# All products of one superchunk before the other, in the first tile of an MLP's up projection

## The chip, the core and the metric

The kernel runs on one core of a Trainium2 chip. The metric is the device time of one execution in microseconds. The engines are TensorE (PE, matrix products), VectorE (DVE), ScalarE (ACT), GpSimd (POOL) and SyncE (SP, which here only issues transfers). Each works through a queue of instructions in a fixed order and waits at semaphores.

## The reference

One layer of a decoder with two mixers, then an MLP, on 1024 prompt tokens and 64 decode tokens (1088 together). Cut to what matters here:

```
h = x + concat([o_r, o_s], axis=-1) @ w_out
hf = rms_norm(h, norm_ffn_gain)
h = h + jnp.square(jax.nn.relu(hf @ w_up)) @ w_down
```

The width is 1024, that of the MLP 4096. All inputs and outputs are float32.

## The kernel before

The tokens are cut into two superchunks of 544 (s = 0 and 1), each with two halves of Q = 272. After the mixers comes the output projection with the residual, superchunk 0 and then 1; `residual` puts h aside, multiplies it by the gain (tile f) and sums its squares (acc). The factor 1/rms is not multiplied into the operand. It is applied behind the up projection: `act` computes max(x, 0) times rsf, and its square on ACT.

The MLP's products follow the scheme with seven products for a 2x2 block product. `up(fp)` computes 256 columns of w_up, fp from 0 to 15 (a tile of up). Its left factors are sums and differences of the four quadrants of the weights: product 1 takes the first quadrant, 2 the second, 4 the fourth, and 5, 6, 7, 3 take combinations (wu0_s5, wu0_s6, ...), which POOL forms in `left`. `wsplit` then splits each into a high part, cast on ACT, and a low part, subtracted on DVE (wu0_w6 is the factor of product 6 of tile 0). The order of the products is `PROD = (1, 2, 6, 5, 7, 4, 3)`. The right operands (op_0h, op_0l for superchunk 0, op_1h, op_1l for 1) are made by `operands` from f and stay for all sixteen tiles.

One product for one superchunk is four times `mm3`, the three matmuls hi x hi, lo x hi, hi x lo: 12 matmuls of 272 columns. Each superchunk has three accumulators in PSUM, psx, psy and psz. Products 1, 6, 7 and 4 add up one after another in psx, 2 stands in psy, 5 and 3 in psz. After 1, 6 and 7 ACT copies the running sum out (tiles m1, m6, m7, shown as m); DVE adds psy or psz to these copies and calls act.

The loads of the weights' halves (wu_r) are issued by ACT's queue, into three buffers; the split factors have four buffers of each of two kinds (wa, wb). The first two factors of tile 0 are made ahead, with the last residuals.

The 1/rms of superchunk s is made in two steps. `norm(s)` sums acc over the partitions with 24 small matmuls (psr), scales on DVE (into rst for s = 0, nsinks for s = 1) and takes the power -1/2 on POOL. `norm_spread(s)` spreads the result over the partitions with six matmuls against the identity (psn), which ACT copies to rsf. For superchunk 0 both lie between residuals of superchunk 1; for superchunk 1 both lie in the first tile of up.

The order of each engine's queue is not simply that of the code: a planner with its own estimate of times sets it, under the dependencies of the code. It runs when the kernel is built.

Of the kernel before, what the change touches and what calls it, by code (L numbers as in the profile page):

```python
# [11 lines left out]
F32 = mybir.dt.float32  # L12
F32R = mybir.dt.float32r
AF = mybir.ActivationFunctionType
ALU = mybir.AluOpType
# [5 lines left out]
P = 128  # L21
# [3 lines left out]
Q = 272  # L25
# [11 lines left out]
def hymba_layer(ctx: ExitStack, tc: tile.TileContext, a: dict, o: dict):  # L37
    nc = tc.nc
# [68 lines left out]
    ident = cload("ident")  # L107
# [21 lines left out]
    u_d = [scratch.tile([P, 2, 2, 7, Q], F32, name=f"u_d{g}") for g in range(8)]  # L129
# [47 lines left out]
    def mm3(ps, lh, ll, rh, rl, first, last, more=False):  # L177
        nc.tensor.matmul(ps, lh, rh, start=first, stop=False, skip_group_check=more)  # L178
        nc.tensor.matmul(ps, ll, rh, start=False, stop=False, skip_group_check=more)  # L179
        nc.tensor.matmul(ps, lh, rl, start=False, stop=last, skip_group_check=more)  # L180
# [120 lines left out]
    for c, (c0, cw) in enumerate(CH):  # L301
        acc = rsb[:, c0 : c0 + cw]
# [4 lines left out]
    w = wload(a["w_in"][2], 8, "wkv", "v")  # L307
# [462 lines left out]
        return raw  # L770


    mix, acc, fs = {}, {}, {}

    def mix_load(s, pl):
        for x, d_ in zip("hl", (ms_hi_d, ms_lo_d)):
# [15 lines left out]
    def out_half(s, half, ps, h, w, first, last):  # L792
        for k in range(4):
            lh, ll = (w[:, i, k * 128 : k * 128 + 128] for i in range(2))
            mh, ml = (mix[s, half + x][:, k, h, :] for x in "hl")
            mm3(ps, lh, ll, mh, ml, first and k == 0, last and k == 3)

    def residual(s, m, pss):
        y = om.tile([P, 2, Q], F32, tag="y", name=f"y{s}_{m}", bufs=2)
# [53 lines left out]
    def norm(s):  # L853

        ps = psM.tile([P, 512], F32, tag="b", name=f"psr{s}")
        for h in range(2):
            for i, r in enumerate((0, 128, 144)):
                col_sums(ps[:, 3 * h + i : 3 * h + i + 1], acc[s][:, h, r : r + 128], ones[:, 0:1])
        rf = (rst, nsinks)[s][:, 0:6]
        nc.vector.tensor_scalar(rf, ps[:, :6], 1.0 / 1024.0, EPS, ALU.mult, ALU.add)  # L860
        rsqrt_inplace(rf, 6)

    def norm_spread(s):
        rf = (rst, nsinks)[s][:, 0:6]
        for h in range(2):
            pb = psM.tile([P, 512], F32, tag="b", name=f"psn{s}{h}")
            for i, (c0, n) in enumerate(((0, 128), (128, 128), (256, 16))):
                nc.tensor.matmul(
                    pb[:, c0 : c0 + n], rf[:, 3 * h + i : 3 * h + i + 1].broadcast_to([P, 128]), ident[:, 128 - n :],
                    start=True, stop=True,  # L870
                )
            nc.scalar.copy(rsf[:, s, h, :], pb[:, :Q])  # L872


# [12 lines left out]
    held = {}  # L887
# [104 lines left out]
    for ms in ((0, 1), (2, 3), (4, 5), (6, 7)):  # L992
        if ms[0] > 3:
            out_parts(1, ms, "a", late, pss)
        out_parts(1, ms, "r", late, pss)
        if ms == (6, 7):
            gen0 = left(PROD, a["w_up"][0], "wu0", nc.vector, tags=("wa", "wa", "wb", "wb"))
            ready = [next(gen0), next(gen0)]
        for m in ms:
            residual(1, m, [pss[m, h] for h in range(2)])  # L1000
            if rest:
                operands(0, rest.pop(0))
            operands(1, m)
        if ms == (2, 3):
            norm(0)
        if ms == (4, 5):
            norm_spread(0)
    ox.close()


# [4 lines left out]
    def up(fp):  # L1015
        gen = chain(ready, gen0) if fp == 0 else left(
            PROD, a["w_up"][fp], f"wu{fp}", nc.vector, tags=("wa", "wa", "wb", "wb"))
        x, y, z = ([bank(f"ps{n}{s}") for s in range(2)] for n in "xyz")
        home = {1: (x, True), 2: (y, True), 6: (x, False), 5: (z, True), 7: (x, False), 4: (x, False), 3: (z, False)}
        ra, rb = ([um.tile([P, n, Q], F32, tag=f"r{n}{s}", name=f"r{n}t{fp}_{s}") for s in range(2)] for n in (3, 4))  # L1020
        held, wait = {}, []

        def tq(n, s):
            return um.tile([P, Q], F32, tag="tq", name=f"{n}{fp}_{s}", bufs=9)

        def add(n, s, bank_):
            t_ = held[n, s]
            nc.vector.tensor_tensor(t_, t_, bank_, ALU.add)
            return t_

        def act(t_, src, s, h, dst):

            nc.vector.scalar_tensor_tensor(t_, src, 0.0, rsf[:, s, h, :], ALU.max, ALU.mult)  # L1033
            nc.scalar.activation(dst, t_, AF.Square)

        for i in PROD:
            w = next(gen)
            for s in range(2):
                bk, first = home[i][0][s], home[i][1]
                for k in range(4):  # L1040
                    lh, ll = (w[:, j, k * 128 : k * 128 + 128] for j in range(2))
                    rh, rl = (ops[RIGHT[i]][s][j][:, k, :] for j in range(2))
                    mm3(bk, lh, ll, rh, rl, first and k == 0, k == 3, not first)
                if i in (1, 6, 7):
                    t_ = held[i, s] = tq(f"m{i}", s)
                    nc.scalar.copy(t_, bk)
                if i == 2:
                    t_ = add(1, s, bk)
                    wait.append((t_, t_, s, 0, ra[s][:, B11, :]))
                    if fp or s == 0:  # L1050
                        act(*wait.pop())
                    else:
                        norm(1)
                if i == 6 and s == 1 and wait:
                    norm_spread(1)
                if i == 7:
                    if wait:
                        act(*wait.pop())
                    t_ = add(7, s, z[s])
                    act(t_, t_, s, 1, ra[s][:, B22, :])  # L1060
                if i == 4:
                    act(tq("v", s), bk, s, 0, ra[s][:, B21, :])
                    nc.sync.dma_start(u_d[fp // 2][:, fp % 2, s, :3, :], ra[s])
                if fp == 15 and s == 1 and i == 2:
                    first_down(1, ("1h", "1l", "2h", "2l"))
                if fp == 15 and s == 1 and i == 5:
                    first_down(6, ("6h", "6l", "5h", "5l"))
                if i == 3:
                    t_ = add(6, s, bk)
                    r12 = um.tile([P, Q], F32, tag="r12", name=f"r12{fp}_{s}", bufs=2)  # L1070
                    act(t_, t_, s, 1, r12)
                    b11, b21, b22 = (ra[s][:, i_, :] for i_ in (B11, B21, B22))
                    t1, t2, t3, t4 = (rb[s][:, i_, :] for i_ in range(4))
                    sub = lambda o_, p_, q_: nc.gpsimd.tensor_tensor(o_, p_, q_, ALU.subtract)  # L1074
                    sub(t1, r12, b11)
                    sub(t2, b22, t1)
                    sub(t4, b21, t2)
                    sub(t3, b22, r12)
                    nc.sync.dma_start(u_d[fp // 2][:, fp % 2, s, 3:, :], rb[s])

    begun, raws1 = {}, []

# [198 lines left out]
```

## Time and profile before

| | |
|---|---|
| median of 3 runs | 1247.72 us (1240.08 to 1247.75) |
| profiled execution | 1244.97 us, span 1243.2 us |
| PE busy | 1199.7 us, 97% of the span |
| DVE, POOL, ACT busy | 69%, 45%, 41% |
| granted clock of PE, mean | 0.982 |

The profiled execution is one of its own beside the three runs. Its span counts from the first to the last instruction. A row of an engine's timeline may stand for several instructions (x3), with the time from the first start to the last end. The first tile of up begins at 530.32 us.

### The profile page before, as it was taken

To read this page: it belongs to the slowest core of one execution; us is meant where nothing else is said; L and a number is where in the kernel's file an instruction comes from. 1 tells how busy PE (TensorE), PEld (TensorE's weight loads), DVE (VectorE), ACT (ScalarE), POOL (GpSimd) and SP (SyncE) were. 2 spreads that over 40 slices of the span, in tenths; PEclk is the share of its full clock that TensorE was granted. 3 is DMA by queue.
4 is the path that set the end of the run, shared out by engine and by line. 5 is a ranking of instruction groups with operands and counts; after the bars stand their busy time and mean duration, and the time that the engine had idled before them with its cause. 6 is when DMAs were issued, how large, how long until landed. Compare 5 with 4: busy or idle time off the path is not lost.

```text
span 1243.2 us, 23934 instructions
## 1 busy us (share of the span) xinstructions
PE 1199.7 (97%) x9621; PEld 1153.0 (93%) x9621; DVE 851.7 (69%) x1508; ACT 507.9 (41%) x1035; POOL 553.5 (45%) x463
## 2 busy tenths in 40 slices
PE   7999999999998999969999999999889999999998
PEld 6999888888888999869999999999889999999998
DVE  8856667643136888778666676766378778897776
ACT  6343434573124425444444444444363424233331
POOL 8425333332225646467666666666472231253000
PEclk9999999999899999979999999999989999999999
DMA  6211235232415753523434343445664445553215
GB/s 235 70 59 65 82 104 159 91 100 75 120 52 181 220 162 114 166 79 141 152 129 150 135 149 135 142 151 176 202 227 144 159 144 175 197 176 125 73 55 180
DMA packets 102277, 169.46 MB, mean 136 GB/s; under 512 B 11999, under 2 KB 68255, under 8 KB 101911
## 3 DMA queue, kind: packets, MB, share of 16 engines
q1 hardware_dynamic: 89335, 124.35, 30.0%
q10 hardware_dynamic: 10272, 34.67, 8.8%
q0 software_dynamic: 2560, 8.91, 2.3%
q8 instruction: 75, 1.23, 0.4%
q14 instruction: 35, 0.29, 0.1%
HBM read 114.30 MB, written 53.61 MB: 135 GB/s over the span
## 4 chain that ended last, share of the span: by engine, by line
PE 56%; DVE 6%; DMA 2%; issue 2%; POOL 1%; ACT 1%; ACTq 0%; DVEq 0%; POOLq 0%
PE psd L179 8%; PE psd L178 8%; PE psd L180 8%; PE psx L178 5%; PE psx L179 5%; PE psx L180 5%; PE psz L178 2%; PE psz L180 2%; PE psz L179 2%; PE pso L178 1%; PE pso L180 1%; PE pso L179 1%; DVE op_0l L755 1%; PE psy L178 1%; PE psy L180 1%
## 5 line engine op out<-in xcount | busy, mean ns | idle before, releaser
L178 PE MATMUL psd<-uh,wd_w 128*128 128x272 f32 x896 | 258.7, 290 | 8.0 <-ACT wd_w L754 4.5
L179 PE MATMUL psd<-uh,wd_w 128*128 128x272 f32 x896 | 260.1, 291 | 0.2 <-DVE wd_w L755 0.2
L180 PE MATMUL psd<-ul,wd_w 128*128 128x272 f32 x896 | 258.6, 289 | 0.0
L178 PEld LDWEIGHTS psd<-uh,wd_w 128*128 128x128 f32 x896 | 169.9, 190 | 9.0 <-ACT wd_w L754 4.7
L179 PEld LDWEIGHTS psd<-uh,wd_w 128*128 128x128 f32 x896 | 169.7, 189 | 0.5 <-DVE wd_w L755 0.5
L180 PEld LDWEIGHTS psd<-ul,wd_w 128*128 128x128 f32 x896 | 169.6, 189 | 0.0
L1151 DVE TENSOR_TENSOR a<-a,psd 128x272 f32<-128x272 f32 x248 | 101.5, 430 | 43.0 <-PE psd L180 42.9
L755 DVE TENSOR_TENSOR wu_w<-wu_s,wu_w 128x512 fp32r<-128x512 f32 x64 | 64.3, 1009 | 53.8 <-ACT wu_w L754 53.2
L755 DVE TENSOR_TENSOR ul<-ur,uh 128x1088 fp32r<-128x1088 f32 x56 | 82.2, 1493 | 11.3 <-ACT uh L754 11.3
L754 ACT CAST wd_w<-wd_s 128x512 fp32r<-128x512 f32 x64 | 37.4, 618 | 119.1 <-PE psd L180 104.5
L178 PE MATMUL psx<-op_0h,wu_w 128*128 128x272 f32 x256 | 75.2, 294 | 7.1 <-ACT wu_w L754 5.2
L180 PE MATMUL psx<-op_0l,wu_w 128*128 128x272 f32 x256 | 74.9, 293 | 0.0
L178 PE MATMUL psx<-op_1h,wu_w 128*128 128x272 f32 x256 | 74.8, 292 | 0.0
L179 PE MATMUL psx<-op_0h,wu_w 128*128 128x272 f32 x256 | 74.7, 292 | 0.0
L180 PE MATMUL psx<-op_1l,wu_w 128*128 128x272 f32 x256 | 74.5, 291 | 0.0
L179 PE MATMUL psx<-op_1h,wu_w 128*128 128x272 f32 x256 | 74.2, 290 | 0.0
L366 POOL TENSOR_TENSOR sp<-sp,ssp 128x1024 f32<-128x1024 f32 (+1 forms) x16 | 28.6, 1787 | 100.4 <-DVE ssp L365 95.7
L1033 DVE SCALAR_TENSOR_TENSOR m<-m,rsf 128x272 f32<-128x272 f32 x96 | 69.3, 722 | 3.2 <-ACT rsf L872 0.6
L754 ACT CAST uh<-ur 128x1088 fp32r<-128x1088 f32 x56 | 59.5, 1099 | 17.8 <-PE psd L179 9.1
L1074 POOL TENSOR_TENSOR r4t<-r3t,r4t 128x272 f32<-128x272 f32 x64 | 64.6, 1019 | 1.2
L755 DVE TENSOR_TENSOR wd_w<-wd_s,wd_w 128x512 fp32r<-128x512 f32 x64 | 52.4, 832 | 16.8 <-ACT wd_w L754 16.8
L178 PE MATMUL psf<-hnh,wqk_hi 128*128 128x384 f32 (+1 forms) x192 | 63.3, 330 | 0.0
(328 smaller groups left out, 3809.2 us busy)
## 6 DMA issues: line engine op xcount, KB each, us to landing
ur<-u_d SPq DMA_DIRECT2D x54, 544.0 KB, 5.0
u_d<-r4t SPq DMA_DIRECT2D x32, 544.0 KB, 4.5
wu_r<-in_w_up ACTq DMA_DIRECT2D x32, 512.0 KB, 4.2
wd_r<-in_w_down ACTq DMA_DIRECT2D x30, 512.0 KB, 5.3
u_d<-r3t SPq DMA_DIRECT2D x32, 408.0 KB, 2.9
y<-in_xY POOLq DMA_DIRECT2D x16, 272.0 KB, 3.1
y_d<-y POOLq DMA_DIRECT2D x16, 272.0 KB, 3.5
yt<-y_d SPq DMA_DIRECT2D x16, 272.0 KB, 3.8
```

The costliest lines, as they stand in the source:

```text
L178: nc.tensor.matmul(ps, lh, rh, start=first, stop=False, skip_group_check=more)
L179: nc.tensor.matmul(ps, ll, rh, start=False, stop=False, skip_group_check=more)
L180: nc.tensor.matmul(ps, lh, rl, start=False, stop=last, skip_group_check=more)
L366: nc.gpsimd.tensor_tensor(s, s, ss.unsqueeze(2).broadcast_to([P, 4, n]), ALU.mult)
L754: nc.scalar.copy(hi, src)
L755: lo_eng.tensor_tensor(lo, src, hi.bitcast(F32), ALU.subtract)
L1033: nc.vector.scalar_tensor_tensor(t_, src, 0.0, rsf[:, s, h, :], ALU.max, ALU.mult)
L1074: sub = lambda o_, p_, q_: nc.gpsimd.tensor_tensor(o_, p_, q_, ALU.subtract)
L1151: nc.vector.tensor_tensor(to, to, ps, ALU.add)
```

## The change

In the first tile (fp = 0) the loop runs over all seven products for superchunk 0 and then over all seven for superchunk 1; the other fifteen tiles keep the order of product by product, both superchunks each. `norm(1)` is called behind product 5 of superchunk 0, and `norm_spread(1)` behind product 4, with its matmuls ordered behind the last matmul of that product. `mm3` returns its last matmul for that. The holding back of superchunk 1's first act (the list `wait`) goes, since its rsf is there before. For norm_spread(0) the tie to the last matmul of the output projection's part ahead of it is new as well; it moves no instruction.

```diff
-    def norm_spread(s):
+    def norm_spread(s, ins):
...
-                nc.tensor.matmul(
+                with tc.issue_after(ins.ins):
+                    nc.tensor.matmul(
...
-        for i in PROD:
-            w = next(gen)
-            for s in range(2):
...
-                if i == 2:
-                    t_ = add(1, s, bk)
-                    wait.append((t_, t_, s, 0, ra[s][:, B11, :]))
-                    if fp or s == 0:
-                        act(*wait.pop())
-                    else:
-                        norm(1)
-                if i == 6 and s == 1 and wait:
-                    norm_spread(1)
-                if i == 7:
-                    if wait:
-                        act(*wait.pop())
...
+        order = [(i, s) for s in range(2) for i in PROD] if fp == 0 else [(i, s) for i in PROD for s in range(2)]
...
+        for i, s in order:
+            if i not in ws:
+                ws[i] = next(gen)
+            w = ws[i]
...
+                ins = mm3(bk, lh, ll, rh, rl, first and k == 0, k == 3, not first)
...
+            if i == 2:
+                t_ = add(1, s, bk)
+                act(t_, t_, s, 0, ra[s][:, B11, :])
+            if fp == 0 and s == 0 and i == 5:
+                norm(1)
+            if fp == 0 and s == 0 and i == 4:
+                norm_spread(1, ins)
```

What the planner makes of it is seen in the queues. On PE the first tile begins with products 1 and 2 of superchunk 0; then come the first matmuls of products 6 and 5, fourteen of the 24 sums, the rest of 6 and 5, the other ten sums, products 7, 4 and 3, the spreading, and superchunk 1 with 1, 2, 5, 6, two blocks of tile 1's product 1, then 7, two blocks of tile 1's product 2, then 4 and 3. From tile 2's second product on, all queues hold the same rows as before.

ACT, from the first copy out of psx in tile 0, before (the number behind a name is the buffer's; m10_0 is the copy after product 1 for superchunk 0, wu1_w1 the factor of product 1 of tile 1):

```order
L1046 COPY m10_0_6086<-psx0_6064 128x272
L1046 COPY m10_1_6100<-psx1_6065 128x272
L1034 ACTIVATE r3t0_0_6070<-m10_0_6086 128x272
L754 CAST wu0_w6_6161<-wu0_s6_6159 128x512
L754 CAST wu0_w5_6202<-wu0_s5_6157 128x512
L754 CAST wu0_w7_6231<-wu0_s7_6229 128x512
L754 CAST wu0_w4_6270<-wu0_r2_6002 128x512
L754 CAST wu1_w1_6366<-wu1_r1_6362 128x512
L754 CAST wu1_w2_6397<-wu1_r1_6362 128x512
L769 DMA wu1_r2_6364<-in_w_up 128x1024
L754 CAST wu0_w3_6307<-wu0_s3_6305 128x512
L769 DMA wu2_r1_6623<-in_w_up 128x1024
```

and ACT from the same copy now:

```order
L1050 COPY m10_0_6086<-psx0_6064 128x272
L1037 ACTIVATE r3t0_0_6070<-m10_0_6086 128x272
L754 CAST wu0_w6_6107<-wu0_s6_6105 128x512
L754 CAST wu0_w5_6124<-wu0_s5_6103 128x512
L754 CAST wu0_w7_6168<-wu0_s7_6166 128x512
L754 CAST wu0_w4_6188<-wu0_r2_6002 128x512
L754 CAST wu0_w3_6219<-wu0_s3_6217 128x512
L769 DMA wu1_r2_6364<-in_w_up 128x1024
L769 DMA wu2_r1_6623<-in_w_up 128x1024
L1050 COPY m60_0_6122<-psx0_6064 128x272
L754 CAST wu1_w6_6434<-wu1_s6_6432 128x512
L1050 COPY m70_0_6183<-psx0_6064 128x272
```

The square of superchunk 0 (the ACTIVATE) stands ahead of the casts in both; the casts of tile 1's first two factors have moved back, the load of its second half has moved up by one cast, and the cast of wu1_w6 now stands ahead of the copy m70_0.

POOL, from its last operation on the right operands (f1), before:

```order
L849 TENSOR_TENSOR f1_7_6038<-f1_7_6038,f1_3_5662 128x272
L971 TENSOR_TENSOR wu0_s5_6157<-wu0_r2_6002 128x512
L971 TENSOR_TENSOR wu0_s6_6159<-wu0_s5_6157,wu0_r1_6000 128x512
L971 TENSOR_TENSOR wu0_s7_6229<-wu0_r1_6000,wu0_r2_6002 128x512
L132 TENSOR_TENSOR nsinks_113<-nsinks_113,mhalf_111 128x6
L971 TENSOR_TENSOR wu0_s3_6305<-wu0_r1_6000,wu0_s6_6159 128x512
L971 TENSOR_TENSOR wu1_s5_6430<-wu1_r2_6364 128x512
```

and POOL from the same operation now:

```order
L849 TENSOR_TENSOR f1_7_6038<-f1_7_6038,f1_3_5662 128x272
L972 TENSOR_TENSOR wu0_s5_6103<-wu0_r2_6002 128x512
L972 TENSOR_TENSOR wu0_s6_6105<-wu0_s5_6103,wu0_r1_6000 128x512
L972 TENSOR_TENSOR wu0_s7_6166<-wu0_r1_6000,wu0_r2_6002 128x512
L972 TENSOR_TENSOR wu0_s3_6217<-wu0_r1_6000,wu0_s6_6105 128x512
L972 TENSOR_TENSOR wu1_s5_6430<-wu1_r2_6364 128x512
L972 TENSOR_TENSOR wu1_s6_6432<-wu1_s5_6430,wu1_r1_6362 128x512
L972 TENSOR_TENSOR wu1_s7_6492<-wu1_r1_6362,wu1_r2_6364 128x512
L972 TENSOR_TENSOR wu1_s3_6566<-wu1_r1_6362,wu1_s6_6432 128x512
L132 TENSOR_TENSOR nsinks_113<-nsinks_113,mhalf_111 128x6
```

The power of the second norm (nsinks) has moved behind the last combination of tile 0 and all four of tile 1.

## Rows read from the trace of the kernel before

**Rows 1.** Waits of PE, 500 to 566 us: who for whom, us in total, times, longest.

```profile
PE psx L178 <- ACT wu_w L754: 5.2, 1, 5.2
PE psy L180 <- DVE op_1l L755: 3.3, 2, 1.7
...
PE psy L178 <- ACT op_1h L754: 1.7, 1, 1.7
```

**Rows 2.** PE's timeline, first tile of up: start, us, instruction, count, idle before and releaser.

```profile
530.32 0.28 PE L178 MATMUL psx<-op_0h,wu_w 128*128 128x272 f32 x1
...
531.83 0.29 PE L178 MATMUL psx<-op_1h,wu_w 128*128 128x272 f32 x1
...
542.77 0.82 PE L158 MATMUL psr<-ones,acc 128*32 128x1 f32 x48
548.75 0.59 PE L178 MATMUL psx<-op_0h,wu_w 128*128 128x272 f32 x1 [5.16 <-ACT wu_w L754]
...
551.90 0.42 PE L180 MATMUL psx<-op_0l,wu_w 128*128 128x272 f32 x1
552.13 0.33 PE L179 MATMUL psx<-op_1h,wu_w 128*128 128x272 f32 x1
...
553.55 1.41 PE L868 MATMUL psn<-c_ident,nsinks 128*128 128x128 f32 x12
554.81 0.37 PE L178 MATMUL psz<-op_0h,wu_w 128*128 128x272 f32 x1
```

**Rows 3.** ACT's timeline there (ACTq: its DMA issues).

```profile
547.76 0.43 ACT L1034 ACTIVATE r3t<-m 128x272 f32<-128x272 f32 x1 [3.58 <-DVE m L1033]
548.09 1.64 ACT L754 CAST wu_w<-wu_s 128x512 fp32r<-128x512 f32 x3
549.64 1.66 ACT L754 CAST wu_w<-wu_r 128x512 fp32r<-128x512 f32 x3
552.34 0.33 ACTq L769 DMA_DIRECT2D wu_r<-in_w_up  x1
...
558.32 1.14 ACT L754 CAST wu_w<-wu_s 128x512 fp32r<-128x512 f32 x2 [2.60 <-POOL wu_s L971]
559.63 0.39 ACT L1046 COPY m<-psx 128x272 f32<-128x272 f32 x1 [0.17 <-PE psx L180]
```

**Rows 4.** DVE's timeline there.

```profile
540.85 5.46 DVE L755 TENSOR_TENSOR op_1l<-f,op_1h 128x272 fp32r<-128x272 f32 x6
546.22 0.77 DVE L1028 TENSOR_TENSOR m<-m,psy 128x272 f32<-128x272 f32 x2
...
548.73 2.98 DVE L755 TENSOR_TENSOR wu_w<-wu_s,wu_w 128x512 fp32r<-128x512 f32 x3 [0.93 <-ACT wu_w L754]
```

**Rows 5.** POOL's timeline there.

```profile
543.12 1.46 POOL L971 TENSOR_TENSOR wu_s<-wu_r 128x512 f32<-128x512 f32 x1
...
547.88 1.35 POOL L132 TENSOR_TENSOR nsinks<-nsinks,mhalf 128x6 f32<-128x6 f32 x1 [0.45 <-DVE nsinks L860]
...
555.63 1.29 POOL L971 TENSOR_TENSOR wu_s<-wu_r 128x512 f32<-128x512 f32 x1 [5.08 <-DMA wu_r<-in_w_up]
...
559.50 1.74 POOL L971 TENSOR_TENSOR wu_s<-wu_r,wu_s 128x512 f32<-128x512 f32 x1
```

**Rows 6.** Tile wu_r, 500 to 640 us: time of its loads from issue to landing.

```profile
DMA to landing us min/median/max: 3.2/4.1/5.7
```

**Rows 7.** PE's timeline at two other waits.

```profile
509.31 0.39 PE L178 MATMUL pso<-mixah,woa 128*128 128x272 f32 x1 [2.98 <-DVE y L802]
...
910.63 0.59 PE L178 MATMUL psd<-uh,wd_w 128*128 128x272 f32 x1 [2.15 <-ACT a L1149]
```

**Rows 8.** Windows behind these two: us, busy us (count) by engine, granted clock, DMA.

```profile
509.30:511.00 1.70, 1.69 (x13) 1.69 (x14) 1.70 (x5) 0.11 (x1) 1.10 (x2) 1.00 0.03 10
...
910.60:912.00 1.40, 1.37 (x6) 1.37 (x7) 1.40 (x2) 0.26 (x1) 1.32 (x2) 0.50 0.58 129
```

**Rows 9.** Waits of PE, 566 to 1243 us.

```profile
PE psd L178 <- ACT wd_w L754: 4.5, 1, 4.5
```

More of the change, by code (lines that the diff above doesn't have):

```diff
@@ L770, in rawload @@
         return raw
[L773 removed]
+    mix, acc, fs, last_out = {}, {}, {}, [None]
     def mix_load(s, pl):
@@ L795, in out_half @@
             mh, ml = (mix[s, half + x][:, k, h, :] for x in "hl")
-            mm3(ps, lh, ll, mh, ml, first and k == 0, last and k == 3)
+            last_out[0] = mm3(ps, lh, ll, mh, ml, first and k == 0, last and k == 3)
     def residual(s, m, pss):
@@ L1006, in hymba_layer @@
         if ms == (4, 5):
-            norm_spread(0)
+            norm_spread(0, last_out[0])
     ox.close()
@@ new lines, in up @@
+        for i, s in order:
+            if i not in ws:
+                ws[i] = next(gen)
+            w = ws[i]
+            bk, first = home[i][0][s], home[i][1]
+            for k in range(4):
+                lh, ll = (w[:, j, k * 128 : k * 128 + 128] for j in range(2))
+                rh, rl = (ops[RIGHT[i]][s][j][:, k, :] for j in range(2))
+                ins = mm3(bk, lh, ll, rh, rl, first and k == 0, k == 3, not first)
+            if i in (1, 6, 7):
+                t_ = held[i, s] = tq(f"m{i}", s)
+                nc.scalar.copy(t_, bk)
+            if i == 2:
[5 more added lines that the diff above has]
+                norm_spread(1, ins)
+            if i == 7:
+                t_ = add(7, s, z[s])
+                act(t_, t_, s, 1, ra[s][:, B22, :])
+            if i == 4:
+                act(tq("v", s), bk, s, 0, ra[s][:, B21, :])
+                nc.sync.dma_start(u_d[fp // 2][:, fp % 2, s, :3, :], ra[s])
+            if fp == 15 and s == 1 and i == 2:
+                first_down(1, ("1h", "1l", "2h", "2l"))
+            if fp == 15 and s == 1 and i == 5:
+                first_down(6, ("6h", "6l", "5h", "5l"))
+            if i == 3:
+                t_ = add(6, s, bk)
+                r12 = um.tile([P, Q], F32, tag="r12", name=f"r12{fp}_{s}", bufs=2)
+                act(t_, t_, s, 1, r12)
+                b11, b21, b22 = (ra[s][:, i_, :] for i_ in (B11, B21, B22))
+                t1, t2, t3, t4 = (rb[s][:, i_, :] for i_ in range(4))
+                sub = lambda o_, p_, q_: nc.gpsimd.tensor_tensor(o_, p_, q_, ALU.subtract)
+                sub(t1, r12, b11)
+                sub(t2, b22, t1)
+                sub(t4, b21, t2)
+                sub(t3, b22, r12)
+                nc.sync.dma_start(u_d[fp // 2][:, fp % 2, s, 3:, :], rb[s])
```

39 lines of the change are left out of this document (5 added, 34 removed).

## The prediction

> **What bounds the kernel now.** I read first who waits for whom on TensorE (PE), before and after 566 us, then the timelines of the four engines around the first tile of up. Up to there and behind it PE runs almost without a break; at this one place it has four waits, 5.2 us for a weight factor and 3.3 and 1.7 us for the right operands of superchunk 1 [rows 1], together 10.2 us. So what the change is worth must be read here.
>
> I call a block one product for one superchunk: 12 matmuls, 1.51 us at the full clock (530.32 to 531.83) [rows 2], 0.126 us a matmul. Tile 0 has 14 blocks. Before, the first four (products 1 and 2, both superchunks) and the norm's sums are done at 543.6; then PE idles until 548.75, because the third factor, w6, is not there [rows 2]. What holds w6 back is worth following. POOL begins the combinations of tile 0 at 543.12 [rows 5]. DVE splits the last right operands until 546.3, then does two additions of product 2 [rows 4]. ACT has the square of superchunk 0 ahead of the cast of w6 in its queue; this waits 3.58 us for DVE and runs at 547.76, the cast begins at 548.09, PE starts 0.66 us later [rows 3]. So ACT works strictly in its order, and w6 comes late through what stands ahead of it, not through PE. From 548.75 PE runs with matmuls 0.23 us apart until 552.13 (the lower clock), then at full rate; the spreading takes 553.55 to 554.81 [rows 2], and the eight remaining blocks of tile 0 follow without a wait: 554.81 + 8 x 1.51 = 566.9 is where tile 0's work ends (one block of tile 1 that stands between is not counted on either side).
>
> **The change part by part.**
>
> *The waits for superchunk 1's operands go.* The blocks of products 1 and 2 for superchunk 1 move behind the spreading, long after their operands. That takes away 3.3 + 1.7 us of waiting. But PE now has only two blocks before w6, not four, so it comes to w6 some 9 us earlier (533 to 534 rather than 543.6), and w6 doesn't come earlier with it. What would be late next is exactly the wait of 5.16 us, grown to some 14.
>
> *When w6 comes.* Nothing ahead of it depends on the moved blocks: POOL's, ACT's and DVE's rows up to the last right operand are the same in both orders. Only the second addition is gone from ahead of the square, half of 0.77 us [rows 4]. So the cast of w6 starts at 547.7 and PE at 548.4. The two blocks taken out of the shadow of this wait, and the sums, now have to be run after it: this is the loss.
>
> *The rest of the first pass.* From 548.4 PE does w6 and w5 with 24 sums among them. The low factor of w6 is there at about 549.4 (a subtraction takes 2.98 / 3 = 0.99 us) [rows 4]. I take the low clock (1.2 GHz) to end as much earlier as PE starts, at 551.8: ten matmuls 0.23 us apart, then twelve at 0.126, the sums 0.8: about 553.6. Product 7: 555.1. At 0.99 us each the other low factors are there at 550.4, 551.4, 552.4 and 553.4, ahead of their blocks. In ACT's queue the issue of tile 2's first load waits for the subtraction of w4 (552.4), and the copy after product 6 for this issue: 552.8, in time for product 7.
>
> *A new wait, at product 4.* Products 7 and 4 write the same bank, and with one superchunk alone they stand next to each other: product 4 can't start until ACT has copied the sum with product 7 out. Before, superchunk 1's block of 1.51 us covers that copy of 0.39 us [rows 3]. Now that copy stands in ACT's queue behind the cast of wu1_w6, tile 1's factor, which waits for POOL's second combination of tile 1, which waits for the load of tile 1's second half. Its issue: five casts of 0.55 us (1.64 / 3, 1.66 / 3) from 547.7, so 550.45, 1.9 us before the 552.34 of now. From issue to the first combination 3.29 us (552.34 to 555.63) [rows 3, 5]: 553.75. To the cast 2.69 us (558.32 - 555.63): 556.45. Cast 0.57 (half of 1.14) and copy 0.39: 557.4. So product 4 waits from 555.1 to 557.4, 2.3 us, and products 4 and 3 end at 557.4 + 3.0 = 560.4. The first 2.3 us of any error ahead of it are hidden by this wait.
>
> *The spreading.* The power of the norm on POOL now stands behind all four combinations of tile 1, not between the third and fourth of tile 0. These take 555.63 to 559.50 + 1.74 = 5.61 us, the power 1.35 [rows 5]: 553.75 + 5.61 + 1.35 = 560.7. PE waits 0.3 us for it, then spreads for 1.26: 562.0. Behind PE's waiting spread all of superchunk 1 is queued, although its matmuls don't need it.
>
> *The second pass.* Seven blocks at 1.51 = 10.6: 572.5. I add no wait: all seven factors are there; between its products 6, 7 and 4 the order puts two blocks of tile 1 each, so the copies are covered again. The first of these needs tile 1's w1 at 562.0 + 4 x 1.51 = 568.0; its buffer is free after superchunk 1's product 1 at 563.5, and copy, cast and subtraction (0.39 + 0.55 + 0.99) give 565.4, so 2.6 us to spare. Reordered stores of the result and the move of tile 2's loads cost nothing, since the blocks of tile 1 (14 x 1.51 = 21 us) cover them.
>
> **Sum.** 572.5 - 566.9 = +5.6 us; the profiled execution's 1244.97 becomes 1250.6. It lies 2.75 below the median of the three runs (1247.72), which run from 1240.08 to 1247.75; on the median the forecast is 1253.3.
>
> **Bounds.** The load is the term with the widest price: 3.2 to 5.7 us, median 4.1 [rows 6]. I take 3.29 because it is the same load at the same place, with the same second load behind it. Product 4 and the power both move with it one for one, so the sum is +5.5 to +8.0. The clock after the new 2.3 us wait is open from both sides. After a wait of 2.98 us at 509.31 it stayed at 1.00 (2.4 GHz); after one of 2.15 at 910.63 it was 0.50 [rows 7, 8]. At 0.50, twelve matmuls 0.10 us longer give +1.2; product 3 then ends behind the power, so 0.3 of it is hidden. A gain here has no row. [...]
>
> **The rivals.**
>
> *The clock falls at product 4's wait.* For it: the row at 910.63, a wait of nearly the same length. Against: the row at 509.31, a longer wait without that cost [rows 7, 8]. +5.6 + 0.9 = +6.5, or 1254.2. [...]
>
> *Faster: the waits go and none grows.* If w6 were cast by 533.3, PE would run tile 0 through: 14 x 1.51 + 0.8 + 1.26 = 23.2 us from 530.32 rather than 36.6, so 13.4 us less, 1234.3. It decides at w6: its combination would have to end 10 us before the first combination of now begins (543.12) [rows 5], and in the new order the same operations on the operands stand ahead of it on POOL. Nearly excluded. Even at half of the gap the case ends within 1%.
>
> *Absorbed.* A later wait of PE that hangs on a transfer and not on PE gives the delay back. The longest is 4.5 us, for a factor of down [rows 9]. If it is paced by something earlier than PE, +5.6 - 4.5 = +1.1, 1248.8. Against it: those factors' buffers are given free by PE's own matmuls.
>
> *Slower by 1%: tile 1's factors late.* All seven factors of tile 0 are now held until the second pass. If w1's subtraction ends after 568.0 (2.6 us later than worked out, as with a slow DVE queue behind the cast of w6), PE meets another empty place of the size of the one of now: 5.16 us and 15 matmuls 0.10 us longer, 6.7 in all. +12.3, with the clock above +13.2: 1260 to 1261.
>
> **How the numbers follow.** The sum as it stands 0.45, with the fallen clock 0.25; absorbed 0.13; tile 1's factors late 0.12; faster 0.05. Predicted 1253.3. The first two with the load's bounds reach from 1253 to 1257. The range reaches to 1246 (absorbed, and runs that lie as far below their median as the profiled execution does) and to 1260. A measurement of this kernel tells about 1% from no change, since its own three runs lie 0.6% apart. By that bound the first three cases count as the same (0.83); faster 0.05; slower 0.12.
>
> **What would show it.** In the new profile: PE idle for about 14 us from 534, ended by ACT's cast of w6 at about 548.4; no wait for op_1; a wait of some 2 us at the block of psx with w4, ended by ACT's copy or cast, with ACT itself waiting for POOL, and POOL for a load; the spreading ended by POOL's power at about 560.7; then no wait until tile 2. It is wrong if w6's cast comes much earlier than 548, if product 4 starts right after product 7, or if the waits behind 600 us differ from those of now.

## The result

| | before | changed |
|---|---|---|
| median of 20 runs each | 1245.61 us (1240.08 to 1249.08) | 1248.39 us (1245.99 to 1251.9) |
| span of the profiled execution | 1243.2 us | 1245.3 us |
| granted clock of PE, mean | 0.982 | 0.986 |

The changed kernel takes 1.0029 of the time before, 95% interval [1.0019, 1.0039]: 1245.61 x 0.0029 = 3.6 us more, 2.4 to 4.9. The forecast was 1253.3, from +5.6 us on a median of three runs (1247.72) that turned out 2.1 us above that of twenty. So the direction and the place were right and the size was too large: of the 4.9 us between 1253.3 and 1248.39, 2.1 lie in that base and 2.8 in the change itself.

The waits of PE from 500 to 566 us, now:

```profile
PE psx L178 <- ACT wu_w L754: 14.0, 1, 14.0
...
PE psx L178 <- ACT m L1050: 0.5, 1, 0.5
```

The three waits for superchunk 1's operands [rows 1] are gone, the one for w6 has grown from 5.2 to 14.0 us, and a new one stands at product 4. PE's timeline of the first tile:

```profile
546.09 0.59 PE L178 MATMUL psx<-op_0h,wu_w 128*128 128x272 f32 x1 [14.00 <-ACT wu_w L754]
546.61 0.59 PE L178 MATMUL psz<-op_0h,wu_w 128*128 128x272 f32 x1
547.13 0.59 PE L158 MATMUL psr<-ones,acc 128*32 128x1 f32 x28
...
551.00 0.43 PE L179 MATMUL psz<-op_0h,wu_w 128*128 128x272 f32 x1
551.22 0.39 PE L180 MATMUL psz<-op_0l,wu_w 128*128 128x272 f32 x1
...
552.30 0.36 PE L158 MATMUL psr<-ones,acc 128*32 128x1 f32 x20
552.59 0.39 PE L178 MATMUL psx<-op_0h,wu_w 128*128 128x272 f32 x1
...
554.84 0.39 PE L178 MATMUL psx<-op_0h,wu_w 128*128 128x272 f32 x1 [0.47 <-ACT m L1050]
...
557.96 1.41 PE L869 MATMUL psn<-c_ident,nsinks 128*128 128x128 f32 x12
559.22 0.37 PE L178 MATMUL psx<-op_1h,wu_w 128*128 128x272 f32 x1
```

PE starts again at 546.09 with w6 and w5, the matmuls 0.23 us apart until 551.2; product 7 begins at 552.59, product 4 at 554.84 after only 0.47 us of wait, and the spreading at 557.96 without one. Seven blocks are left: 559.22 + 7 x 1.51 = 569.8.

Absolute times don't compare here. POOL begins its first combination of tile 0 at 540.46 (the rows below begin with its fourth), against 543.12 before [rows 5], though the queues ahead of it hold the same rows; two more profiles have 542.83 (the changed kernel again) and 540.90 (the kernel before again). So I count the tile from this combination to the end of its 14 blocks. It took 566.93 - 543.12 = 23.8 us before and 569.82 - 540.46 = 29.4 now, +5.6; with the second profiles 24.6 and 30.0, so +5.5 by the means.

ACT's timeline (ACTq: its DMA issues) and POOL's:

```profile
545.10 0.43 ACT L1037 ACTIVATE r3t<-m 128x272 f32<-128x272 f32 x1 [3.86 <-DVE m L1036]
545.43 1.12 ACT L754 CAST wu_w<-wu_s 128x512 fp32r<-128x512 f32 x2
546.23 0.33 ACTq L769 DMA_DIRECT2D wu_r<-in_w_up  x1
546.46 0.61 ACT L754 CAST wu_w<-wu_s 128x512 fp32r<-128x512 f32 x1
546.98 0.61 ACT L754 CAST wu_w<-wu_r 128x512 fp32r<-128x512 f32 x1
547.50 0.61 ACT L754 CAST wu_w<-wu_s 128x512 fp32r<-128x512 f32 x1
...
552.15 0.62 ACT L754 CAST wu_w<-wu_s 128x512 fp32r<-128x512 f32 x1 [1.21 <-POOL wu_s L972]
554.40 0.39 ACT L1050 COPY m<-psx 128x272 f32<-128x272 f32 x1 [1.63 <-PE psx L180]
```

```profile
544.73 1.46 POOL L972 TENSOR_TENSOR wu_s<-wu_r,wu_s 128x512 f32<-128x512 f32 x1
549.48 1.27 POOL L972 TENSOR_TENSOR wu_s<-wu_r 128x512 f32<-128x512 f32 x1 [3.29 <-DMA wu_r<-in_w_up]
...
555.00 1.35 POOL L132 TENSOR_TENSOR nsinks<-nsinks,mhalf 128x6 f32<-128x6 f32 x1
```

The load of tile 1's second half is issued at 546.23, 0.04 us after POOL's last combination of tile 0 ends (544.73 + 1.46), and ahead of three casts that stand before it in ACT's queue. Before, the same issue came at 552.34 [rows 3], 0.03 us after DVE's subtraction of w4 (551.63 + 0.68). So it seems that the load now takes the buffer that POOL's last combination frees; the experiment with the load late, below, puts it back behind the subtraction. The load lands so early that the cast of wu1_w6 (552.15) is over when product 7 ends: the copy (554.40) waits for PE and for nothing else. From issue to the first combination it is 3.25 us, against 3.29 [rows 3, 5].

### The profile page after: what moved, and what is told of

It is laid out like the page before. It is cut to its first block, busy times and chain, and to the rows that moved or that the text cites. A ratio compares the mean times of both kernels' runs of the same rounds, so it can differ in the third digit from the quotient of the medians.

```text
span 1245.3 us, 23934 instructions
## 1 busy us (share of the span) xinstructions
PE 1194.7 (96%) x9621; PEld 1146.6 (92%) x9621; DVE 849.6 (68%) x1508; ACT 508.2 (41%) x1035; POOL 554.4 (45%) x463
## 4 chain that ended last, share of the span: by engine, by line
PE 63%; DVE 7%; DMA 4%; issue 2%; ACT 2%; POOL 1%; ACTq 0%; SPq 0%; DVEq 0%; POOLq 0%
PE psd L179 8%; PE psd L180 8%; PE psd L178 8%; PE psx L178 5%; PE psx L179 5%; PE psx L180 5%; PE psz L178 2%; PE psz L180 2%; PE psz L179 2%; PE pst L178 1%; PE pst L179 1%; PE pst L180 1%; PE pso L179 1%; PE pso L178 1%; PE pso L180 1%
## 5 line engine op out<-in xcount | busy, mean ns | idle before, releaser
L755 DVE TENSOR_TENSOR wu_w<-wu_s,wu_w 128x512 fp32r<-128x512 f32 x64 | 60.8, 954 | 53.6 <-ACT wu_w L754 52.7
```

The costliest lines, as they stand in the source:

```text
L755: lo_eng.tensor_tensor(lo, src, hi.bitcast(F32), ALU.subtract)
```

## The experiments

My theory (L): w6 comes when it comes, paced by the work on the operands and by the square ahead of its cast; the change takes two blocks out of the wait for it, and they are run behind it. Its rival (Q): the cost lies behind w6, at the copy after product 7 and at the spreading. In the table "restart" is from POOL's first combination to PE's start with w6; "low clock" is how long the granted clock (one-microsecond windows from the restart) was 0.50, a window in between counted in proportion; "tile" is as above. "At 880" is the wait for ACT's copy about 880 us, and "down" the time from the end of the longest wait at the start of down (about 903 us) to the end of the span; both come up further below. All are from one profile each and in us; ratios are to the kernel before, with 95% intervals.

| kernel | ratio | wait for w6 | restart | low clock | tile | at 880 | down |
|---|---|---|---|---|---|---|---|
| before | | 5.16 | 5.63 | 3.4 | 23.8 | 1.95 | 339.5 |
| before, again | 0.9997 [0.9982, 1.0013] | 5.17 | 5.63 | 5.3 | 24.6 | 2.24 | 340.2 |
| changed | 1.0029 [1.0019, 1.0039] | 14.00 | 5.63 | 5.4 | 29.4 | 0.28 | 341.9 |
| changed, again | 1.0043 [1.0028, 1.0058] | 13.99 | 5.63 | 6.7 | 30.0 | 0.46 | 342.2 |
| one block back | 0.9982 [0.9966, 0.9999] | 11.00 | 5.62 | 4.6 | 26.6 | 0.4 | 338.6 |
| two blocks back | 1.0014 [0.9999, 1.0030] | 5.91 | 5.63 | 6.8 | 26.1 | 0.31 | 343.3 |
| changed, square late | 1.0027 [1.0010, 1.0043] | 11.96 | 3.58 | 6.5 | 28.4 | 0.39 | 342.0 |
| before, square late | 0.9990 [0.9974, 1.0005] | 3.12 | 3.59 | 3.7 | 21.9 | 2.04 | 339.3 |
| the same again | 0.9970 [0.9958, 0.9983] | 3.11 | 3.58 | 5.4 | 22.7 | 2.08 | 337.7 |
| changed, sums early | 1.0004 [0.9989, 1.0019] | 6.35 | 5.03 | 5.5 | 28.2 | 0.28 | 340.1 |
| two blocks back, sums early | 0.9973 [0.9960, 0.9985] | 5.16 | 5.62 | 6.2 | 25.6 | 0.42 | 340.2 |
| these two, square late | 0.9959 [0.9943, 0.9974] | 3.12 | 3.58 | 5.2 | 23.3 | 0.4 | 338.4 |
| changed, load late | one run | 14.20 | 5.62 | 7.1 | 30.1 | 0.4 | 341.2 |
| changed, row moved | 1.0008 [0.9996, 1.0020] | 14.0 | 5.62 | 4.7 | 29.1 | 0.35 | 338.5 |
| before, row moved | 0.9991 [0.9974, 1.0008] | 5.2 | 5.63 | 4.7 | 24.4 | 2.10 | 339.3 |
| two blocks back, row moved | 0.9985 [0.9971, 0.9999] | 5.9 | 5.62 | 5.8 | 25.7 | 0.33 | 339.7 |
| all three edits, row moved | 0.9976 [0.9963, 0.9988] | 3.1 | 3.59 | 4.6 | 23.0 | 0.56 | 340.0 |

**Both kernels once more, no edit.**

> The changed kernel once more, for a second profile and a second ratio. I measure tile 0 from the start of POOL's first combination (the chain that makes w6) to the end of its 14 blocks: 23.8 us before (543.12 to 566.9), 29.4 after (540.46 to 569.8). Theory L (w6 comes late and is not moved; two blocks and the sums now stand behind it): 29.4 again within 0.5, with PE idle 13 to 15 us. The stretch ahead of the first combination was 2.7 us shorter in the profile of after than in that of before, though no instruction there changed places. If that was chance, it lies anywhere between 540 and 544 this time; if it is 540.5 again, something systematic ahead of the tile belongs to the change, and the time of +0.3% would be 5.6 less 2.7. Rival Q (the cost stands behind w6, at product 4 and at the spreading): waits of more than 1 us there.

> The kernel before once more: a second profile of tile 0 and the ratio of a kernel to itself. From the start of POOL's first combination to the end of the 14 blocks: 23.8 us within 0.5, low clock for 3 to 4 us behind the wait for w6; ratio 1.000 within its interval. If tile 0 is 25 or more, the difference of 5.6 to 6.2 between before and after is partly chance.

The wait for w6 repeats to 0.01 us; the low clock behind it doesn't (5.4 and 6.7, 3.4 and 5.3 us in kernels with not one row different), nor does the first combination's place. A single span can't tell +3 from +6 us here.

**Two blocks back.** The order of the first tile begins with products 1 and 2 for both superchunks, and is the changed one from there on; superchunk 1's first act waits for the spreading, as before.

```diff
+        order = [(1, 0), (2, 0), (1, 1), (2, 1)] + [(i, s) for s in range(2) for i in PROD[2:]] if fp == 0 else ...
```

> The change, but products 1 and 2 run for both superchunks before product 6, as before; from there superchunk 0 goes on alone. Superchunk 1's first act waits for the spreading. Theory L: two blocks of 1.51 us go back into the shadow of the wait for w6, so tile 0 from POOL's first combination is 29.4 - 3.0 = 26.4 us, with the waits for op_1 back inside it and PE idle some 3 us less; time about 0.25% under the change, no better than before. Rival Q: the two blocks shift what stands behind them, tile 0 stays within 1 us of 29.4.

The tile fell from 29.4 and 30.0 to 26.1, near L's 26.4 and not within Q's one microsecond. PE's row at the restart:

```profile
549.29 0.59 PE L178 MATMUL psx<-op_0h,wu_w 128*128 128x272 f32 x1 [5.91 <-ACT wu_w L754]
```

The wait is 5.91 in place of 14.00, and the restart comes at the same 5.63 us after the combination. The operands' waits (1.68 and 1.86) are back as well, and they cost nothing, since PE waits for w6 behind them anyway. This is the point of the whole case: two blocks ahead of w6 are free, behind it they cost their 3.0 us. That the tile is still 1.5 to 2.3 us longer than before (26.1 against 24.6 and 23.8) fits the sums, 0.8 us, that here stand behind w6, and a low clock of 6.8 us against 5.3 and 3.4, of which half is lost.

**One block back.** Product 1 for superchunk 1 alone stands ahead of w6.

```diff
+        order = [(1, 0), (2, 0), (1, 1)] + [(i, 0) for i in PROD[2:]] + [(i, 1) for i in PROD[1:]] if fp == 0 else ...
```

> The changed kernel with one block of superchunk 1 (product 1) put back ahead of w6. If the loss is the work taken out of w6's shadow, PE restarts 5.6 us after POOL's first combination as in all others, the wait for w6 is 9 to 11 us, and the first tile takes one block less than in the changed kernel, 27.9 to 28.5 us, halfway to the 26.1 us with two blocks put back; ratio 1.001 to 1.003. If the loss lies behind w6 (the copy after product 7, the spreading), it stays at 29.4 to 30 us, whatever stands ahead of w6.

The wait came to 11.00, as L has it, and the restart stayed; the tile (26.6) is below both expectations, and so is the ratio (0.9982, for 1.001 to 1.003). The order accounts for a part of it: the planner also drew superchunk 1's block of product 6 ahead of the spreading, between products 7 and 4, where it covers the copy (PE has no wait at product 4), and the low clock was among the shortest of the changed orders. So this run speaks against Q, but it is no clean middle dose.

**The square behind the casts.** `halve` keeps its two instructions in `split`; superchunk 0's addition, multiplication and square are placed behind the split of w5 in the queues, with the data as they were. In the kernel before, superchunk 1's addition, the power and the spreading change their places with them. For the changed kernel:

```diff
+            if i == 5 and fp == 0 and s == 0:
+                with tc.issue_after(split[0].ins), tc.issue_after(split[1].ins):
+                    t_ = add(1, s, y[s])
+                    act(t_, t_, s, 0, ra[s][:, B11, :])
```

> The change, but the addition and the act of product 2 for superchunk 0 (DVE and ACT) are tied behind the splitting of w5, so they don't stand ahead of the cast of w6. Theory L: the cast starts when POOL's second combination ends, 2.9 us after the start of the first and not 5.0; PE starts 2.1 us earlier. From there the load of tile 1's second half and the power, which don't move, take part of it back (product 4's copy behind the cast of wu1_w6, 0.4 us; the spreading behind the power, 0.4): tile 0 is 27.9 us, -1.5. Rival Q: those two take all of it, 29.4.

> The kernel before, with the same tie: both additions and superchunk 0's act of product 2 stand behind the splitting of w5, the power of the second norm directly behind the second combination, the spreading behind product 6. Theory L: PE starts 2.1 us earlier and nothing else is late, so tile 0 from the first combination is 21.7 us rather than 23.8, and the kernel 0.15 to 0.2% faster than before. Rival Q: no change, 23.8.

> The kernel before with the addition and act of product 2 tied behind the splitting of w5, once more, to settle whether it beats the kernel before: its ratio was 0.999 [0.9974, 1.0005], its tile 0 21.9 us. Theory L: tile 0 of 21.5 to 22.3 again, ratio 0.998 to 0.999. Rival: 1.000, the gain lost to what varies ahead of the tile.

The restart came 2.05 us sooner in all of them (3.58 and 3.59 for 5.63), and the tile followed: 28.4 for 29.4 and 30.0, and 21.9 and 22.7 for 23.8 and 24.6. So the square was what held the cast of w6 back, by two of the five microseconds that PE waited before, and what the prediction read from [rows 3] is shown. In the kernel before it gives 0.9970 in one comparison and no measurable gain in the other, with intervals that overlap.

**The sums ahead of the wait.** In all profiles the low clock seemed longer where the 24 short sums followed the wait. I put them ahead of product 6, into the wait, and their power on POOL behind the combinations.

```diff
                 ws[i] = next(gen)
+                if fp == 0 and i == 6:
+                    norm(1)
...
             if fp == 0 and s == 0 and i == 5:
-                norm(1)
+                norm_power()
```

> The change, but the second norm's sums are taken out ahead of product 6, so that PE does them while it waits for w6, and the power stands behind the second combination. Tile 0 of the change was 29.4 and 30.0 us. Theory S (the sums cost more than their 0.8 us, since with them right behind the wait PE stayed at the low clock for 5.2 to 6.8 us and not 3.3 to 3.6): -0.8 and -1 to -2.5, so 27 to 28. Rival C (how long the low clock lasts is chance): -0.8 alone, 28.6 to 29.2, the low clock anywhere from 3 to 7 us.

> As the kernel with products 1 and 2 run for both superchunks first (tile 0 of 26.1 us), and the sums ahead of product 6 as well. What then is left of the change is the order from product 6 on and the place of the spreading. Theory S: 26.1 - 0.8 - 1.5 = 23.8, as before the change; the loss is then accounted for by the two blocks and by the sums with the low clock behind them. Rival C: 25.3. Rival Q (waits behind w6): 25.3 or more, with waits of PE at product 4 or the spreading.

The low clock stayed: 5.5 and 6.2 us, with no sums behind the wait. The theory that they prolong it falls, and what sets its length stays open. What is saved in the tile is about the sums' own time with two blocks back (26.1 to 25.6, near C's 25.3). In the changed kernel the tile fell to 28.2, between the two expectations, and 0.6 us of that is a restart that came sooner (5.03 for 5.63): DVE's multiplication ahead of the square took 0.44 us there, for 1.04, and the rest of the way to w6 is the same. The ratios fell more than that, from 1.0014 to 0.9973, 5 us; the last group of experiments shows where most of that lies.

**All three together**, two blocks back with the sums early and the square late.

> All three edits that gained alone, together: products 1 and 2 of both superchunks first, the second norm's sums ahead of the wait for w6, and superchunk 0's multiplication and square moved behind the casts of w6 and w5 in the queues. If the gains add, the cast of w6 no longer waits for the square, so PE restarts 3.6 us after POOL's first combination rather than 5.6; the first tile, counted from that combination, takes 23.0 to 24.2 us (25.6 with the sums moved, less 2.0), and the wait at 880 us stays at 0.3 to 0.5 us: 0.995 to 0.997 of before. The rival is that the square's move brings nothing here, because something else holds w6 back as long: the first tile stays at 25.6 us and the ratio at 0.997 to 0.998.

The gains add in the tile (23.3). PE's row, and ACT's, where the square (547.40) now stands behind the casts of w6 and w5:

```profile
545.45 0.60 PE L178 MATMUL psx<-op_0h,wu_w 128*128 128x272 f32 x1 [3.12 <-ACT wu_w L754]
...
554.71 0.39 PE L178 MATMUL psx<-op_0h,wu_w 128*128 128x272 f32 x1 [0.48 <-ACT m L1061]
```

```profile
544.78 1.14 ACT L754 CAST wu_w<-wu_s 128x512 fp32r<-128x512 f32 x2 [1.85 <-POOL wu_s L981]
547.40 0.43 ACT L1046 ACTIVATE r3t<-m 128x272 f32<-128x272 f32 x1 [1.48 <-DVE m L1045]
```

At 0.9959 [0.9943, 0.9974], 1239.95 us (six runs), it is faster than both kernels, and its ratio is the lowest of all that I ran; the intervals of 0.9970 and 0.9973 in the table overlap with it. It still works superchunk 0 through its products ahead of superchunk 1's, except for the two blocks that fill the wait.

**The load late.** A copy of two columns out of wu0_r1, put in ACT's queue behind product 7's copy, makes the load of tile 1's second half take the other buffer. PE's, DVE's and SP's queues hold the same rows as in the changed kernel; POOL's power moves ahead of one combination.

```diff
+                    with tc.issue_after(split[0].ins):
+                        nc.scalar.copy(tq("d", 0)[:, :2], raw_now[0][:, :2])
```

> The changed kernel with a copy of two columns out of the raw weights wu0_r1 placed in ACT's queue behind product 7's copy; by it the load of tile 1's second half takes the other buffer, whose last reader is DVE's subtraction of w4. PE's and DVE's queues stay the same. If that load's issue is what moves product 4's wait, its issue comes 2.5 us after PE's restart rather than 0.1, the cast of wu1_w6 some 8.4 us after the restart rather than 6.1, and the copy after product 7 stands behind it: product 4 starts 9.4 us or more after the restart and waits 0.5 to 1.3 us, by how long the low clock lasts; not the 2.3 us that were predicted, because the load starts before w4's subtraction ends in neither case. The rival, that the copy never stands behind the cast, gives 0.47 us as in the changed kernel, with the cast ended long before.

ACT's rows, and DVE's subtraction of w4:

```profile
551.46 0.33 ACTq L771 DMA_DIRECT2D wu_r<-in_w_up  x1
...
557.35 0.62 ACT L754 CAST wu_w<-wu_s 128x512 fp32r<-128x512 f32 x1 [3.55 <-POOL wu_s L975]
558.00 0.39 ACT L1056 COPY m<-psx 128x272 f32<-128x272 f32 x1
```

```profile
550.74 0.68 DVE L755 TENSOR_TENSOR wu_w<-wu_r,wu_w 128x512 fp32r<-128x512 f32 x1
```

The issue came 2.51 us after the restart (548.95), at the end of that subtraction (550.74 + 0.68), and the cast 8.40 us after it, both as expected. But the low clock lasted 7.1 us, product 7 ended as the cast did, and product 4 waited 0.47 us, as in the changed kernel. So the chain behind the load is shown in its length, and a wait longer than 0.47 isn't: a low clock of this length hides it.

**One row of ACT's queue at the start of down.** The times don't follow the tiles: two blocks back has a tile of 26.1 us and a ratio of 1.0014, one block back 26.6 and 0.9982. What differs is the stretch "down". There the planner placed the issue of one load, wd7_r1, among the eight copies of the sum a1 on ACT's queue: ahead of all with two blocks back, behind one copy in the changed kernel, behind two before, behind three with one block back and with all three edits. All other rows there are the same. With two blocks back ACT's rows and PE's are:

```profile
912.78 0.33 ACTq L769 DMA_DIRECT2D wd_r<-in_w_down  x1
913.16 0.39 ACT L1152 COPY a<-psd 128x272 f32<-128x272 f32 x1 [2.91 <-DVE wd_w L755]
```

```profile
913.60 0.60 PE L178 MATMUL psd<-uh,wd_w 128*128 128x272 f32 x1 [4.99 <-ACT a L1152]
```

The issue waits for a subtraction of DVE until 912.78, the copies behind it with it, and PE 4.99 us for a copy. In four kernels I placed this one row behind the eighth copy and left all other rows of all engines as they were.

```diff
+        if name == "wd7_r1":
+            with tc.issue_after(a1[7].ins):
+                nc.scalar.dma_start(raw, src)
```

> One row is moved, in the changed kernel: on ACT's queue the issue of the load wd7_r1 goes from behind the first copy of down's sum a1 to behind the eighth; all other rows of all engines stay. Theory D: this issue waits for a subtraction on DVE, the copies behind it wait with it, and PE waits for the copies; the change moved it forward by one copy, and so gave the start of down 2 us more. Then the waits for copies a behind the 4.6 us wait fall from 4.4 and 2.5 us to 1 or less, the stretch from that wait to the end from 342 to 338 to 339.5 us, and the ratio from 1.0029 and 1.0043 to 1.000 to 1.002. The rival is that these waits and the low clock there are chance: 342 us and the ratio of the changed kernel.

> The same row moved in the kernel before, there from behind the second copy. By theory D less is to be had, since two copies stand ahead of the issue already: the stretch falls from 339.5 and 340.2 to 338 to 339.5 us, the ratio is 0.998 to 1.000; and between this kernel and the changed one with the same row moved there are the first tile's +5.4 us less the 1.7 us at 880 us, 3 to 4.5 us. By the rival it stays at 1.000 and the difference to the other is that of the kernels as they were.

> The same row moved in the kernel with two blocks back, where it stood ahead of all eight copies and the wait for them was 5.0 us. Theory D: the largest gain of the four, the stretch from 343.3 to 338 to 339.5 us, the ratio from 1.0014 to 0.997 to 0.999. The rival: 343 us and 1.0014.

> The same row moved in the kernel with the three edits together, where three copies stood ahead of it. Theory D: little is left to gain, the waits for copies fall from 1.5 us to 1 or less, the stretch stays at 338 to 338.5 us, and the ratio at 0.994 to 0.997. By the rival the ratio is the same, so this run tells nothing between the two; it is run for the version that beats both kernels.

In the changed kernel seven of ACT's eight copies now begin ahead of the issue, and PE waits once for them, 0.98 us (ACT, then PE):

```profile
911.71 2.09 ACT L1153 COPY a<-psd 128x272 f32<-128x272 f32 x7
913.47 0.33 ACTq L771 DMA_DIRECT2D wd_r<-in_w_down  x1
```

```profile
912.14 0.39 PE L178 MATMUL psd<-uh,wd_w 128*128 128x272 f32 x1 [0.98 <-ACT a L1153]
```

The stretch fell from 341.9 and 342.2 to 338.5, and the ratio from 1.0029 and 1.0043 to 1.0008; with two blocks back from 343.3 to 339.7 and from 1.0014 to 0.9985, where the wait fell to 1.81 only. So this row is shown to be the cause of some 3 us in these two. The waits are only a part of it. In the first 30 us of the stretch (windows of 3 us) PE idles 4.4 and 2.5 us in the two profiles of the changed kernel and 1.0 with the row moved; the granted clock below 1.00 takes, by the share that is missing, 3.2 and 5.1 us there and 2.8 with the row moved. In the kernel before and with all three edits, with two and three copies ahead of it already, nothing was gained that can be measured: 0.9991, and 0.9976 [0.9963, 0.9988] beside 0.9959 [0.9943, 0.9974]. There theory D missed in detail: PE's longest wait for a copy was 2.44 us in the kernel before with the row moved, for 2.15, and with all three edits it was 1.19, the stretch 340.0 for 338 to 338.5, and the ratio above 0.994 to 0.997.

Over all seventeen profiles the stretch follows the place of this row. It is 343.3 us with no copy ahead of the issue (one profile), 341.2 to 342.2 with one (four), 337.7 to 340.2 with two (five), 338.4 to 340.2 with three (three), and 338.5 to 340.0 with the row moved behind the eighth (four).

## Why the prediction held in the tile and failed in the time

The step that failed is the last of the sum: it takes the tile's +5.6 us as the kernel's, with what follows the tile at no change. The runs showed two places behind 600 us where PE's waits differ, which is one of the signs of being wrong that the prediction names: -1.7 us at 880 us, and some +2 us at the start of down. Within the tile the mis-sized term is the wait at product 4, 0.47 us for 2.3. The base, the median of three runs, lay 2.1 us too high as well. Term by term:

**w6.** Predicted: it comes with the second addition saved, 0.35 us earlier. Measured: not earlier; the restart is 5.63 us after the first combination in both kernels. The addition is gone, but the multiplication behind it took 1.04 us, where it took 0.80 before; why was not tried. From the first addition to the square it is 1.54 us in both (546.22 to 547.76 [rows 3, 4]; 543.56 to 545.10 here):

```profile
543.56 0.42 DVE L1031 TENSOR_TENSOR m<-m,psy 128x272 f32<-128x272 f32 x1
544.02 1.04 DVE L1036 SCALAR_TENSOR_TENSOR m<-m,rsf 128x272 f32<-128x272 f32 x1
```

and the multiplication before:

```profile
546.92 0.80 DVE L1033 SCALAR_TENSOR_TENSOR m<-m,rsf 128x272 f32<-128x272 f32 x1
```

That the square holds w6, that nothing of the moved blocks does, and that the wait grows to 14 us was right, and two blocks back show what it costs.

**The rest of the first pass**, "the low clock to end as much earlier as PE starts". This was 5.2 us from the restart to product 7's block (548.4 to 553.6) and measured 6.5 (546.09 to 552.59) and 7.1. The windows of the changed kernel (us, busy by engine, clock, DMA):

```profile
546.09:547.09 1.00, 1.00 (x2) 0.57 (x2) 1.00 (x2) 1.00 (x3) 0.10 (x1) 0.50 0.00 0
...
550.09:551.09 1.00, 1.00 (x6) 1.00 (x6) 0.00 (x0) 0.39 (x1) 0.92 (x2) 0.50 0.96 356
551.09:552.09 1.00, 1.00 (x9) 1.00 (x8) 0.00 (x0) 0.00 (x0) 1.00 (x2) 0.82 0.24 90
...
554.84:556.34 1.50, 1.50 (x12) 1.50 (x13) 0.86 (x2) 0.43 (x1) 1.50 (x2) 1.00 0.00 0
```

0.50 is 1.2 GHz, and it stood for 5.4 us rather than the 3.4 that I had read from the one profile of before; a second profile of before has 5.3.

**The new wait at product 4** is the term of the sum that was mis-sized: 2.3 us predicted, 0.47 and 0.48 measured. Two things made it so. I held the load back behind five casts (2.05 us after the restart), because ACT's computing rows run strictly in its order; it left 0.14 us after the restart. Here the issue didn't wait for the casts ahead of it to run: it left when POOL's last combination had ended, which gives the last of those casts its input. The Trainium skill, Perfetto Trace Analysis, section "DVE / Act Engine Instruction (TENSOR_ADD, Activation, etc)", has a step that fits: once an instruction is in the engine's wait queue, the sequencer is ready for the next. The trace agrees, with 546.23 for the issue and 546.46 to 547.50 for the casts. The other thing is the low clock: product 7 ended 8.3 us after the restart for 6.7 predicted, and 2 us more at half the clock are some 1.0 of these 1.6 us. This second thing is the larger: by these numbers, with the load as late as I had it, product 4 would begin at 9.0, 0.7 us behind product 7's end, and with the load later still (the experiment with the load late) the wait was 0.47 us all the same. As I had written, an error of up to 2.3 us ahead of that wait is hidden by it, and so it went: product 4 begins 8.75 us after the restart, for 9.0 predicted.

**The spreading and the second pass.** 0.3 us of wait predicted, none measured: the power ended at 556.35. Seven blocks without a wait: right. With the errors against each other, the tile came to +5.6 (first profiles) and +5.5 (means of two), for +5.6 predicted. This sum is right by its whole, not by its terms, and that is luck.

**From the tile to the time.** I had counted what follows the tile at no change, because the blocks of tile 1 would cover the reordered stores and loads, and two places answered. At about 880 us, in the last tile of up, PE waits for ACT's copy, and this copy stands behind a cast that waits for the read-back of an earlier result (ur). Before, and now (PE, then ACT):

```profile
882.36 0.40 PE L178 MATMUL psx<-op_0h,wu_w 128*128 128x272 f32 x1 [1.95 <-ACT m L1046]
872.83 0.60 ACTq L1091 DMA_DIRECT2D ur<-u_d  x1
880.92 1.10 ACT L754 CAST uh<-ur 128x1088 fp32r<-128x1088 f32 x1 [5.74 <-DMA ur<-u_d]
```

```profile
883.56 0.39 PE L178 MATMUL psx<-op_0h,wu_w 128*128 128x272 f32 x1 [0.28 <-ACT m L1050]
875.40 0.55 ACTq L1091 DMA_DIRECT2D ur<-u_d  x1
882.12 1.11 ACT L754 CAST uh<-ur 128x1088 fp32r<-128x1088 f32 x1 [4.26 <-DMA ur<-u_d]
```

From issue to cast it is 8.1 us before and 6.7 now. The wait is 2.0 to 2.2 us in all five profiles with before's first tile and 0.3 to 0.6 in all twelve others: 1.7 us are given back, against the change's loss. Behind it, to the wait at 903 us, it is 21.3 us in three of those five (before among them) and 19.9 in the other two and in all twelve. In the 21.3 the granted clock falls behind the wait:

```profile
882.36:885.36 3.00, 3.00 (x16) 3.00 (x17) 3.00 (x7) 1.19 (x3) 0.00 (x0) 0.65 0.34 101
885.36:888.36 3.00, 3.00 (x21) 3.00 (x20) 1.28 (x3) 1.74 (x4) 0.00 (x0) 0.78 0.53 213
```

The other place is the start of down, where the change cost some 2 us, by the experiments above through the row that the planner moved (the part on the change says that all queues hold the same rows from tile 2's second product on; for this one row of ACT's that is wrong). Two waits for copies now, one of 2.15 us before [rows 7]:

```profile
910.52 0.39 PE L178 MATMUL psd<-uh,wd_w 128*128 128x272 f32 x1 [2.47 <-ACT a L1149]
913.60 0.59 PE L178 MATMUL psd<-uh,wd_w 128*128 128x272 f32 x1 [1.95 <-ACT a L1149]
```

The account by the profiles, two of each kernel: tile +5.5 (29.7 less 24.2), then -1.8 to 880 us, -0.7 to 903 (19.9 less 20.6) and +2.1 to the end (342.0 less 339.9): +5.1. The comparisons have +3.6 (2.4 to 4.9) and 1244.85 x 0.0043 = +5.4 (3.5 to 7.2). With the row moved in both kernels there remain 1.0008 - 0.9991 = 0.0017, 2.1 us and by the two intervals -0.5 to 4.7, where I had expected 3 to 4.5. So the forecast's +5.6 lies above the first comparison and within the second, and single microseconds of the account aren't settled.

**The rivals.** That the clock falls at product 4's wait: not put to the test, as the wait was 0.47 us; the clock behind it was 1.00 (the last window above). Absorbed: not by the wait that I named, 4.5 us before [rows 9] and 4.6 now, but in part, 1.7 us or more, by the one at 880. Tile 1's factors late, and faster: neither came, and PE has no wait between 566 and 880 us.

## What to carry to other kernels

When a step is moved away from the front of a wait, look first at whether it was running in the wait's shadow: waits that stand ahead of a longer one cost nothing, and taking them away gains nothing unless what ends the last one comes earlier too. The gain lay there, in the one instruction (the square) that stood ahead of the cast in ACT's queue without need. And where a planner sets the order, one row that it moves some 350 us further on can be worth as much as the change: look through the queues to their end, at what each issue waits for and what stands behind it.

## What the runs showed of the hardware that was not expected

- A DMA issue on ACT's queue left at 546.23 us, before three casts ahead of it in the queue had begun (546.46, 546.98, 547.50). One that had to wait for a subtraction (until 912.78) held up the copies behind it on the same queue.
- After the wait for w6 the granted clock stood at 0.50 for 3.4 to 7.1 us, and for 3.4 and 5.3 in two executions of the same program. Neither the wait's length (3.1 to 14.2 us) nor the sums behind it explain it. The five profiles with before's first tile have 3.4 to 5.4 (mean 4.5), the twelve others 4.6 to 7.1 (mean 5.8), so a part of the order in it isn't excluded.
- The same load of ur, issued behind the same transfers, took 8.1 or 6.7 us to its cast, always the one in before's order and the other in the others. In before's order ACT issues it 0.76 us after SP's store begins (872.07 to 872.83), in the other 0.47 (874.93 to 875.40). That the earlier issue is the cause was not tried. The order of the first tile's stores on SP is not: with two blocks back and the sums early it is that of before, and the load is the short one.
